# A two-layer trunk: the four shifts of V's first half issued together into two slots, and the first head pair's scores two blocks later

## The chip, the cores and the metric

One core of one Trainium2 chip. The time is that of the device, in microseconds (us), from the first to the last work of one launch; the median of several executions counts. One profiled execution gives the trace from which all durations are read. Engines are named as in the profile: PE multiplies matrices (PEld loads its weights), ACT and DVE work on rows of 128 partitions, POOL fills buffers and issues the shift transfers, SP issues the loads from memory. Each engine takes its instructions strictly in the order in which they stand in its queue.

## The reference

The program is a two-layer trunk over 512 tokens of width 1024. The part that matters here is the token mixer of layer 0, a stick-breaking attention with 16 heads of 64:

```python
def stick_breaking_attention(q, k, v):
    ...
        z = jnp.einsum('bhtd,bhsd->bhts', q[:, :, q0:kend], k[:, :, :kend]) * scale
        before = s_idx < t_idx
        log_beta = jax.nn.log_sigmoid(z)
        log_1m = jnp.where(before, jax.nn.log_sigmoid(-z), 0.0)
        later = lax.cumsum(log_1m, axis=3, reverse=True) - log_1m
        a = jnp.where(before, jnp.exp(log_beta + later), 0.0)
        outs.append(jnp.einsum('bhts,bhsd->bhtd', a, v[:, :, :kend]))

def stick_breaking_mixer(h, w_qkv, w_o):
    qkv = (h @ w_qkv).reshape(B, S, 3, SB_HEADS, SB_HEAD_DIM)
    ...
    return o.transpose(0, 2, 1, 3).reshape(B, S, D) @ w_o
```

Before and after it stand RMS norms with a shift, a scale and a gate computed from a vector `c` (`silu(c) @ w + b`); a SwiGLU, a second mixer and another SwiGLU follow.

## The kernel before

**Numbers.** Every float32 operand of a product is split into a high and a low part (`split`: ACT copies the high part, DVE subtracts it for the low part) and a product is three matmuls (`mm3`: high by high, high by low, low by high). A weight comes from memory as `raw` (512 KB, two buffers), and ACT makes `wh` and DVE `wl` of it (five pairs of buffers). So the next load but one can be issued only when DVE has written `wl` of a weight, and a `wh` can be written only when PE has read the weight five places earlier.

**The stage.** V = h·w_v is made in two halves of 512 columns. Each half has eight steps k (`v_step`: 12 matmuls, four token blocks of three) into four PSUM banks. While the first half is made, so are q and k of the first head pair. After it, `v_evac` copies the four banks to `vf` on ACT. Then comes the second half, again eight steps; then the weights of the further head pairs are used as filler (`fill`: q and k of pair 1, 2, ... in `pqk`, eight steps of three matmuls each), between which the attention of the pairs is spread.

**U.** The sum over values works on differences of neighbouring rows, U[t] = V[t+1] − V[t]. A row lives in a partition, so the shift by a row is a transfer from SBUF to SBUF, issued by POOL: one of 127 rows and, but for the last block, one of the single row from the next block (`shifted`). Then DVE subtracts (`vs<-vs,vf`), ACT writes the high part of U and DVE the low part. Before the change, `u_steps` is a generator with one buffer `vs` for all four blocks, taken in the order 2, 3, 0, 1: a block's shift is issued only when the block before has left the buffer.

**Scores.** `scores` makes z for blocks of keys in three groups (B31: keys 3 and 1, 12 matmuls; B2: six; B0: six) into two banks `zb`. ACT reads them into `ga` (a sigmoid) and DVE runs the scan `left<-ga`. All three groups of pair 0 share the two banks and the one buffer `ga`. The bank `zb[0]` also serves, between B0 and the next pair, the sums of the vectors that scale the norms: `z<-acch`, `z<-accl` (one pair of matmuls for each half of G), after which DVE writes G from the bank. `acch` and `accl` are again a high part by ACT and a low part by DVE, in one buffer each.

**Order.** Python code gives the order in which work is offered; a scheduler then sets each engine's queue. From `pe["chain"]` on, PE keeps the code's order; from `dve.chain` on, so does DVE for all but the weights' `wl`. Before that, a U step is only tied behind the last `wl`. Buffers of 4 KB a partition come from one pool of 28 slots (`slot`), among them U, hT, q, k, `vf`, G and A.

**Names.** A is the next of the scaling vectors: DVE adds `rawada` rows into it, one 512 KB load each, from two buffers; the third and fourth of these loads wait for the first and second sum. In the profile L93 is `mm`, L101 a transpose, L116 and L69 are the two halves of `split` and all other DVE work of the helper, L155/L156 and L160/L161 the `wh`/`wl` of a weight (q and k weights of later pairs, all others), L110 a load by SP, L636/L638 the two shift transfers, L888 the sigmoid.

Of the kernel before, what the change touches and what calls it, by code (L numbers as in the profile page):

```python
# [8 lines left out]
F32 = mybir.dt.float32  # L9
F32R = mybir.dt.float32r  # L10
AF = mybir.ActivationFunctionType
ALU = mybir.AluOpType

P = 128
T = 512
NT = T // P
# [15 lines left out]
def trunk(ctx: ExitStack, tc: tile.TileContext, A: dict, out: bass.AP):  # L32
    nc = tc.nc
# [5 lines left out]
    npool = ctx.enter_context(tc.tile_pool(name="npool", bufs=2))  # L39
# [9 lines left out]
    def nm(s):  # L49
        uid[0] += 1  # L50
        return f"{s}_{uid[0]}"

    def slot(dt, name, a=2, b=512):
        return s4.tile([P, a, b], dt, tag="s4", name=nm(name))

    def bank(name, tag="b"):
        return psum.tile([P, 512], F32, tag=tag, bufs=6 if tag == "b" else 2, name=nm(name))
# [19 lines left out]
    dve = Vector()  # L77
# [7 lines left out]
    def order(b, before):  # L85
        tc.add_manual_dep(
            b.ins, before.ins.name,
            mybir.DependencyInfo(mybir.DependencyClass.NoSync, mybir.DependencyReason.DATA),
            reason="order",
        )  # L90
# [21 lines left out]
    def split(hi, lo, src, hi_dve=False):  # L112
        if hi_dve:
            dve.tensor_copy(hi, src)
        else:
            act.activation(hi, src, AF.Copy)  # L116
        dve.tensor_tensor(lo, src, hi.bitcast(F32), ALU.subtract)
# [6 lines left out]
    last_low = [None]  # L124
# [107 lines left out]
    def wget(src, look=3):  # L232

        n = taken[0]
        taken[0] += 1
        while len(got) < min(n + 1 + look, len(stream)):
            wemit()
        assert stream[n][3] == src, (stream[n][3], src)
        return got[n]
# [336 lines left out]
    def ada_step(n=1):  # L576
        bg.step(bg0.step(n))
# [38 lines left out]
    U = [[slot(F32R, "U", 4, 256) for _ in range(NT)] for _ in range(2)]  # L616

    def v_step(vb, hf, k, w):
        for tt in range(NT):
            a, b = hTk(hT, k, tt * P, P)  # L620
            mm3(vb[tt][:], a, b, w[0][:, k % 2, :], w[1][:, k % 2, :], k == 0, k == KD - 1)

    def v_evac(vb, tile2):
        vf = [tile2() for _ in range(2)]
        vf = [vf[tt // 2][:, tt % 2, :] for tt in range(NT)]
        for tt in range(NT):
            act.activation(vf[tt], vb[tt][:], AF.Copy)
        return vf

    def u_steps(vf, hf, pool):  # L630

        def shifted(tt):
            vs = pool.tile([P, 512], F32, tag="vs", name=nm("vs"))
            if tt == NT - 1:
                nc.gpsimd.memset(vs[96:P, :], 0.0)
            nc.gpsimd.dma_start(out=vs[0 : P - 1, :], in_=vf[tt][1:P, :])  # L636
            if tt < NT - 1:
                nc.gpsimd.dma_start(out=vs[P - 1 : P, :], in_=vf[tt + 1][0:1, :])  # L638
            return vs

        turns = (2, 3, 0, 1)
        vs = shifted(turns[0])
        yield
        for n, tt in enumerate(turns):
            b = dve.tensor_tensor(vs[:], vs[:], vf[tt], ALU.subtract)
            if not dve.chain:
                order(b, last_low[0])
            src = vs[:].rearrange("p (a e c) -> p a e c", a=4, e=2)
            dst = U[hf][tt][:].rearrange("p a (q c) -> p a q c", q=4)
            split(dst[:, :, 0::3, :], dst[:, :, 1:3, :], src)  # L650
            if n + 1 < NT:
                vs = shifted(turns[n + 1])
            yield

    onec = oneb[:, 0:1]

# [72 lines left out]
    vb = [bank("v0") for _ in range(NT)]  # L729
# [37 lines left out]
    st0.__exit__(None, None, None)  # L767
    fwork["raw"] = ctx.enter_context(tc.tile_pool(name="wraw2", bufs=2))
    vf0 = v_evac(vb, lambda: slot(F32, "vf"))
    o8 = []  # L770
    with tc.tile_pool(name="att", bufs=1) as att, tc.tile_pool(name="att2", bufs=2) as att2:

# [49 lines left out]
        def fill(n, at=None):  # L822
            for j in range(n):
                next(fgen, None)
                if at is not None and j in [min(a, n - 1) for a in at]:
                    ada_step()
# [3 lines left out]
        B31, B2, B0 = (3, 1), (2,), (0,)  # L830
        gaps = {}
        for js in (B31, B2, B0):
            at, n = {}, 0
# [118 lines left out]
        evac_k(0, pk0)  # L952
        LATE = ((2, (2,)), (3, (2, 3)))
        EARLY = ((0, (0,)), (1, (0, 1))), ((2, (0, 1)), (3, (0, 1)))
        early_u = u_steps(vf0, 0, att)
        next(early_u)
        vb = [bank("v1") for _ in range(NT)]
        zb = [bank("z") for _ in range(2)]
        bg0.bank = bg.bank = lambda: zb[0]
        cur = attend(0)  # L960
        for k in range(KD):
            if k % 2 == 0:
                wv = wget(("wv", 1, k // 2))
            v_step(vb, 1, k, wv)
            if k in (1, 4):
                cur[0](B31 if k == 1 else B2)
            if k in (1, 2, 6):
                ada_step()
            if k in (3, 5, 7):
                next(early_u)  # L970
        next(early_u)
        late_u = u_steps(
            v_evac(vb, lambda: npool.tile([P, 2, 512], F32, tag="n", name=nm("vf"))), 1, att
        )
        next(late_u)
        dve.chain = True
        tw = [bank("tw") for _ in range(2)]
        av = [bank("av") for _ in range(2)]
# [4 lines left out]
        for i in range(NPAIR):  # L983
            scores, flip, values, gather, part = cur
            more = i + 1 < NPAIR
            F = iter(FILLS if i < 5 else LAST[i - 5])
            flip(LATE, 0)
            flip(LATE, 1)
            if i:
                last_part()  # L990
            fill(next(F))
            if more:
                cur = attend(i + 1)
                cur[0](B31)
            fill(next(F), (1,))
            values(LATE, 0, False)
            values(LATE, 1, False)
            fill(next(F))
            flip(EARLY[0], 0)
            flip(EARLY[0], 1)  # L1000
            if i < 4:
                next(late_u)
            fill(next(F))
            if more:
                cur[0](B2)
            fill(next(F), (1,))
            values(EARLY[0], 0, False)
            values(EARLY[0], 1, False)
            flip(EARLY[1], 0)
            flip(EARLY[1], 1)  # L1010
            fill(next(F))
            if more:
                cur[0](B0)
            fill(next(F), (1,) if i > 3 else ())
            values(EARLY[1], 0, True)
            values(EARLY[1], 1, True)
            gather()
            last_part = part
# [521 lines left out]
```

## Time and profile before

| | us |
|---|---|
| median of 3 runs | 1162.52 |
| lowest, highest | 1162.12, 1162.67 |
| the profiled execution's own time | 1165.49 |
| its span, first to last instruction | 1163.7 |

| engine | busy us | share |
|---|---|---|
| PE | 1126.9 | 97% |
| DVE | 933.8 | 80% |
| ACT | 596.9 | 51% |
| POOL | 30.0 | 3% |

The profiled execution is 3.0 us above the median of the runs; durations come from it. The stage of the change lies between 58 and 131 us of a span of 1163.7 us. A row of the timeline has the start, the duration, engine, line, operation, tiles and, in brackets, how long the engine sat idle before it and what ended that. A matmul's duration is that of its way through the array; the distance of two starts is what it costs in a dense row. The mean granted clock of PE over the span was 0.988.

### The profile page before, as it was taken

To read this page: it belongs to the slowest core of one execution; us is meant where nothing else is said; L and a number is where in the kernel's file an instruction comes from. 1 tells how busy PE (TensorE), PEld (TensorE's weight loads), DVE (VectorE), ACT (ScalarE), POOL (GpSimd) and SP (SyncE) were. 2 spreads that over 40 slices of the span, in tenths; PEclk is the share of its full clock that TensorE was granted. 3 is DMA by queue.
4 is the path that set the end of the run, shared out by engine and by line. 5 is a ranking of instruction groups with operands and counts; after the bars stand their busy time and mean duration, and the time that the engine had idled before them with its cause. 6 is when DMAs were issued, how large, how long until landed. Compare 5 with 4: busy or idle time off the path is not lost.

```text
span 1163.7 us, 18665 instructions
## 1 busy us (share of the span) xinstructions
PE 1126.9 (97%) x7436; PEld 1015.0 (87%) x7436; DVE 933.8 (80%) x1215; ACT 596.9 (51%) x985; POOL 30.0 (3%) x55
## 2 busy tenths in 40 slices
PE   7996899999999999999999999999999999999997
PEld 4774788778999999998878898988999999999996
DVE  4964799975998898879677966668979898789996
ACT  6343456564655555545242643626555555565652
POOL 0101000000000000001000000000000000000000
PEclk9987999999999999999999999999999999999999
DMA  8853624313423444327887465224243433222243
GB/s 327 322 170 121 206 97 138 127 56 127 145 92 128 145 146 145 127 90 258 287 278 244 157 239 170 90 89 156 100 143 130 131 141 128 92 91 91 91 144 111
DMA packets 51644, 176.52 MB, mean 152 GB/s; under 512 B 6106, under 2 KB 9434, under 8 KB 51556
## 3 DMA queue, kind: packets, MB, share of 16 engines
q1 hardware_dynamic: 48996, 166.94, 42.6%
q0 software_dynamic: 2560, 8.39, 1.9%
q8 instruction: 58, 0.95, 0.3%
q14 instruction: 30, 0.25, 0.1%
HBM read 164.82 MB, written 8.39 MB: 149 GB/s over the span
## 4 chain that ended last, share of the span: by engine, by line
PE 80%; DMA 8%; DVE 7%; ACT 3%; issue 2%; SPq 0%; DVEq 0%; POOL 0%; ACTq 0%
PE r L93 32%; PE y L93 8%; PE v L93 8%; PE pqk L93 6%; DMA rawada<-in_ada 5%; PE X L93 4%; PE gu L93 4%; PE Y L93 3%; PE u L93 3%; PE z L93 2%; PE av L93 2%; PE W L93 1%; PE Z L93 1%; PE tw L101 1%; DVE wl L161 1%
## 5 line engine op out<-in xcount | busy, mean ns | idle before, releaser
L93 PE MATMUL r<-Sh,wh 128*128 128x256 f32 x608 | 172.1, 283 | 0.0
L93 PE MATMUL r<-Sl,wh 128*128 128x256 f32 x608 | 172.1, 283 | 0.0
L93 PE MATMUL r<-Sh,wl 128*128 128x256 f32 x608 | 172.1, 283 | 0.0
L93 PE MATMUL y<-wh,as 128*128 128x512 f32 x480 | 150.7, 391 | 0.1
L160 ACT ACTIVATE wh<-raw 128x1024 fp32r<-128x1024 f32 x87 | 91.6, 1058 | 113.3 <-PE y L93 58.3
L161 DVE TENSOR_TENSOR wl<-raw,wh 128x1024 fp32r<-128x1024 f32 x87 | 105.8, 1219 | 43.0 <-ACT wh L160 42.6
L116 ACT ACTIVATE wh<-f 128x1024 fp32r<-128x1024 f32 x87 | 92.2, 1060 | 91.0 <-PE r L93 66.5
L69 DVE TENSOR_TENSOR wl<-f,wh 128x1024 fp32r<-128x1024 f32 x87 | 106.2, 1220 | 40.1 <-ACT wh L116 40.0
L93 PEld LDWEIGHTS r<-Sh,wh 128*128 128x128 f32 x608 | 116.7, 192 | 0.0
L93 PEld LDWEIGHTS r<-Sl,wh 128*128 128x128 f32 x608 | 116.7, 192 | 0.0
L93 PEld LDWEIGHTS r<-Sh,wl 128*128 128x128 f32 x608 | 116.7, 192 | 0.0
L93 PEld LDWEIGHTS y<-wh,as 128*128 128x128 f32 x480 | 90.1, 188 | 18.9 <-DVE G L69 0.5
L93 PE MATMUL y<-wl,as 128*128 128x512 f32 x240 | 93.7, 390 | 0.0
L93 PE MATMUL r<-hTh,wh 128*128 128x256 f32 x304 | 87.8, 292 | 0.0
L93 PE MATMUL r<-hTl,wh 128*128 128x256 f32 x304 | 85.4, 282 | 0.0
L93 PE MATMUL r<-hTh,wl 128*128 128x256 f32 x304 | 81.0, 283 | 0.0
L93 PE MATMUL r<-hTh,b 128*128 128x256 f32 x304 | 61.0, 283 | 0.0
L93 PEld LDWEIGHTS r<-hTh,wh 128*128 128x128 f32 x304 | 58.0, 191 | 2.5 <-DVE gu L69 0.8
L93 PEld LDWEIGHTS r<-hTl,wh 128*128 128x128 f32 x304 | 58.1, 191 | 0.1
L116 ACT ACTIVATE wh<-rawx 128x1024 fp32r<-128x1024 f32 x38 | 40.3, 1060 | 34.7 <-PE r L93 31.8
L93 PEld LDWEIGHTS r<-hTh,wl 128*128 128x128 f32 x304 | 55.9, 191 | 0.0
L93 PE MATMUL v<-wh,hTh 128*128 128x512 f32 x128 | 51.6, 403 | 3.8 <-ACT wh L160 2.0
(268 smaller groups left out, 2986.7 us busy)
## 6 DMA issues: line engine op xcount, KB each, us to landing
rawada<-in_ada SPq DMA_DIRECT2D x80, 512.0 KB, 4.4
rawy<-in_wy SPq DMA_DIRECT2D x38, 512.0 KB, 3.5
rawx<-in_wx SPq DMA_DIRECT2D x38, 512.0 KB, 4.1
raw<-in_wdown SPq DMA_DIRECT2D x22, 512.0 KB, 4.5
raw<-in_wdn SPq DMA_DIRECT2D x22, 512.0 KB, 3.5
raw<-in_wqk SPq DMA_DIRECT2D x16, 512.0 KB, 4.1
ada<-in_ada0p SPq DMA_DIRECT2D x12, 512.0 KB, 8.0
raw<-in_wgu SPq DMA_DIRECT2D x12, 512.0 KB, 3.6
```

Source lines behind the costliest of these rows:

```text
L69: b = getattr(nc.vector, op)(*args, **kw)
L93: b = nc.tensor.matmul(o, l, r, start=start, stop=stop, skip_group_check=True)
L101: last_tp[0] = nc.tensor.transpose(o, i, ident)
L116: act.activation(hi, src, AF.Copy)
L160: act.activation(h[:], raw[:], AF.Copy)
L161: last_low[0] = nc.vector.tensor_tensor(l[:], raw[:], h[:].bitcast(F32), ALU.subtract)
```

## The change

The generator is dissolved into two functions, `shifted` (the transfers of one block) and `u_step` (the subtraction and the split of one block). Three things move:

- For V's first half two more slots of the shared pool hold all four shifted blocks (`vs0`), and all seven transfers are issued in a row right after `v_evac`.
- In V's second half the scores of pair 0 stand after step 3 and step 5 (were 1 and 4), and the four U steps after steps 4, 5, 6 and 7 (were 3, 5, 7 and behind the loop).
- V's second half keeps its one buffer and its order; only the code that says so is another.

```diff
+    TURNS = (2, 3, 0, 1)
+    def shifted(vf, tt, vs):
+        if tt == NT - 1:
+            nc.gpsimd.memset(vs[96:P, :], 0.0)
+        nc.gpsimd.dma_start(out=vs[0 : P - 1, :], in_=vf[tt][1:P, :])
+        if tt < NT - 1:
+            nc.gpsimd.dma_start(out=vs[P - 1 : P, :], in_=vf[tt + 1][0:1, :])
+        return vs
+    def u_step(vf, hf, tt, vs):
+        b = dve.tensor_tensor(vs, vs, vf[tt], ALU.subtract)
...
     vf0 = v_evac(vb, lambda: slot(F32, "vf"))
+    vs0 = [slot(F32, "vs") for _ in range(2)]
+    vs0 = {tt: shifted(vf0, tt, vs0[tt // 2][:, tt % 2, :]) for tt in TURNS}
...
-        early_u = u_steps(vf0, 0, att)
-        next(early_u)
...
-            if k in (1, 4):
-                cur[0](B31 if k == 1 else B2)
+            if k in (3, 5):
+                cur[0](B31 if k == 3 else B2)
             if k in (1, 2, 6):
                 ada_step()
-            if k in (3, 5, 7):
-                next(early_u)
-        next(early_u)
-        late_u = u_steps(
-            v_evac(vb, lambda: npool.tile([P, 2, 512], F32, tag="n", name=nm("vf"))), 1, att
-        )
-        next(late_u)
+            if k > 3:
+                tt = TURNS[k - 4]
+                u_step(vf0, 0, tt, vs0[tt])
+        vf1 = v_evac(vb, lambda: npool.tile([P, 2, 512], F32, tag="n", name=nm("vf")))
+        def shifted1(n):
+            vs = att.tile([P, 512], F32, tag="vs", name=nm("vs"))
+            return shifted(vf1, TURNS[n], vs[:])
+        vs1 = shifted1(0)
...
             if i < 4:
-                next(late_u)
+                u_step(vf1, 1, TURNS[i], vs1)
+                vs1 = shifted1(i + 1) if i < 3 else None
```

ACT's queue at the start of V's second half, from the last `k` of pair 0 on (`acch` is the high part of G's first half, `ga<-z` the sigmoid of the scores B31). Before:

```order
L116 ACTIVATE k_125_623<-pk_75_288 128x512
L116 ACTIVATE acch_170_853<-G_102_455 128x512
L888 ACTIVATE ga_613<-z_131_633 128x128
L888 ACTIVATE ga_613<-z_131_633 128x384
L888 ACTIVATE ga_613<-z_132_634 128x128
L160 ACTIVATE wh_137_643<-raw_136_641 128x1024
L888 ACTIVATE ga_613<-z_132_634 128x384
L160 ACTIVATE wh_140_649<-raw_139_647 128x1024
```

Now:

```order
L116 ACTIVATE k_127_633<-pk_75_288 128x512
L116 ACTIVATE acch_168_851<-G_102_455 128x512
L160 ACTIVATE wh_138_650<-raw_137_648 128x1024
L160 ACTIVATE wh_141_656<-raw_140_654 128x1024
L160 ACTIVATE wh_144_662<-raw_143_660 128x1024
L155 ACTIVATE wh_147_693<-raw_146_691 128x1024
L116 ACTIVATE U_25_139<-vs_118_589 128x4x2x64
L885 ACTIVATE ga_623<-z_132_640 128x128
L885 ACTIVATE ga_623<-z_132_640 128x384
L885 ACTIVATE ga_623<-z_133_641 128x128
L885 ACTIVATE ga_623<-z_133_641 128x384
```

Three of the four sigmoids stood ahead of the weight of steps 2 and 3, and the fourth ahead of that of steps 4 and 5; now the weights of steps 2 to 7, a later one and the first U stand ahead of all four.

DVE's queue up to the scores B0 (`left<-ga` 128x1025) and the writing of G. Before:

```order
L69 TENSOR_TENSOR vs_153_782<-vs_153_782,vf_115_582 128x512
L156 TENSOR_TENSOR wl_180_907<-raw_168_843,wh_179_906 128x1024
L69 TENSOR_TENSOR U_23_137<-vs_153_782,U_23_137 128x4x128
L69 TENSOR_TENSOR vs_157_819<-vs_157_819,vf_115_582 128x512
L69 TENSOR_TENSOR U_24_138<-vs_157_819,U_24_138 128x4x128
L69 TENSOR_TENSOR accl_171_854<-G_102_455,acch_170_853 128x512
L69 SCALAR_TENSOR_TENSOR left_121_616<-ga_613,ones_119_608 128x1025
L69 TENSOR_TENSOR G_102_455<-z_131_633,g_169_851 128x512
```

Now:

```order
L69 TENSOR_TENSOR vs_117_588<-vs_117_588,vf_115_582 128x512
L69 SCALAR_TENSOR_TENSOR left_125_628<-ga_623,ones_120_613 128x513
L69 TENSOR_TENSOR U_24_138<-vs_117_588,U_24_138 128x4x128
L69 TENSOR_TENSOR accl_169_852<-G_102_455,acch_168_851 128x512
L156 TENSOR_TENSOR wl_165_838<-raw_155_790,wh_164_837 128x1024
L156 TENSOR_TENSOR wl_178_905<-raw_166_841,wh_177_904 128x1024
L69 SCALAR_TENSOR_TENSOR left_123_626<-ga_623,ones_121_618 128x1025
L69 TENSOR_TENSOR G_102_455<-z_132_640,g_167_849 128x512
```

The low part `accl` still stands behind the last U, with two weights now between it and the scan of B0.

SP's queue of loads, at G's factor `g` and the start of A. Before:

```order
L110 DMA raw_168_843<-in_wqk 128x1024
L110 DMA raw_181_910<-in_wqk 128x1024
L110 DMA raw_190_956<-in_wqk 128x1024
L110 DMA g_169_851<-in_post_g 128x1024
L110 DMA A_174_888<-in_adab 1x1024
```

Now:

```order
L110 DMA raw_166_841<-in_wqk 128x1024
L110 DMA g_167_849<-in_post_g 128x1024
L110 DMA A_172_886<-in_adab 1x1024
L110 DMA raw_179_908<-in_wqk 128x1024
L110 DMA raw_188_954<-in_wqk 128x1024
```

Two weights (k of pair 3 and q of pair 4) that were loaded ahead of `g` and A now stand behind them; A's load waits for a fill of A that POOL does behind the seven transfers. All else, on every engine from the next head pair on, stands as it stood.

More of the change, by code (lines that the diff above doesn't have):

```diff
@@ L628, in v_evac @@
         return vf
[L630 to L653, printed above, removed]
+    TURNS = (2, 3, 0, 1)
[8 more added lines that the diff above has]
+        b = dve.tensor_tensor(vs, vs, vf[tt], ALU.subtract)
+        if not dve.chain:
+            order(b, last_low[0])
+        src = vs.rearrange("p (a e c) -> p a e c", a=4, e=2)
+        dst = U[hf][tt][:].rearrange("p a (q c) -> p a q c", q=4)
+        split(dst[:, :, 0::3, :], dst[:, :, 1:3, :], src)
     onec = oneb[:, 0:1]
```

## The prediction

> **What bounds the kernel now.** First the page: PE is busy almost throughout, so only time in which PE stands still, or runs at a lower clock, can be won. Then the waits of PE over the whole span, longest first (engine, what it waited for, us in total, times, longest).
>
> ```profile
> span 1163.7 us, 18665 instructions
> PE 1126.9 (97%) x7436; PEld 1015.0 (87%) x7436; DVE 933.8 (80%) x1215; ACT 596.9 (51%) x985; POOL 30.0 (3%) x55
> PE z L93 <- DVE accl L69: 8.6, 1, 8.6
> PE v L93 <- ACT wh L160: 2.0, 1, 2.0
> PE z L93 <- DVE k L69: 1.7, 1, 1.7
> PE z L93 <- ACT ga L888: 1.6, 2, 1.3
> ```
>
> The longest wait of all, for `accl`, lies in the stage that is changed; so do the next two rows and most of the fourth. The timeline of PE tells where, and what it costs.
>
> ```profile
> 67.16 0.39 PE L93 MATMUL v<-wh,hTl 128*128 128x512 f32 x1
> 67.48 1.13 PE L93 MATMUL z<-k,q 64*128 64x128 f32 x12
> 70.60 0.51 PE L93 MATMUL v<-wh,hTh 128*128 128x512 f32 x1 [1.98 <-ACT wh L160]
> 71.86 0.80 PE L93 MATMUL v<-wl,hTh 128*128 128x512 f32 x1 [0.76 <-DVE wl L161]
> 82.58 0.39 PE L93 MATMUL v<-wh,hTl 128*128 128x512 f32 x1
> ...
> 94.77 0.50 PE L93 MATMUL pqk<-hTh,wh 128*128 128x512 f32 x1
> 97.05 0.50 PE L93 MATMUL z<-acch,ones 128*128 128x512 f32 x1 [1.32 <-ACT ga L888]
> 106.12 0.80 PE L93 MATMUL z<-accl,ones 128*128 128x512 f32 x1 [8.57 <-DVE accl L69]
> 108.42 0.63 PE L93 MATMUL pqk<-hTl,wh 128*128 128x512 f32 x1
> 108.85 0.63 PE L93 MATMUL pqk<-hTh,wl 128*128 128x512 f32 x1
> 112.47 0.40 PE L93 MATMUL pqk<-hTh,wh 128*128 128x512 f32 x1
> ```
>
> There are two holes. The first opens after step 1 of V's second half: PE waits 1.98 + 0.76 us for the weight of step 2. The second opens behind the scores B0: 1.32 + 8.57 us. After each, matmuls start 0.43 us apart (108.42 to 108.85) for a while. The chain of waits has the dense distance (24 matmuls in 5.44 us, 0.227 each) and what fed the second hole:
>
> ```profile
> 62.11 5.44 PE v L93 x24
> 67.55 1.10 PE z L93 x12
> 82.97 0.55 PE z L93 x6
> 93.94 0.90 PE z L93 x6
> 95.77 1.22 DVE wl L156
> 97.88 0.53 POOL vs L636
> 98.41 4.86 DMA vs<-vf
> 104.11 0.64 ACT U L116
> 105.39 0.69 DVE accl L69
> 116.58 4.91 DMA rawada<-in_ada
> 122.89 4.96 DMA rawada<-in_ada
> 131.07 1.08 PE av L93 x7
> ```
>
> DVE stands in order: `accl` is behind the fourth U, this behind the fourth shift, and that could be issued (97.88) only when the third U had left the one buffer. The granted clock by stretch (us, busy times of the engines, clock, DMA share, GB/s) shows why the dense rows are slow after a hole:
>
> ```profile
> 61.00:66.00 5.00, 5.00 (x23) 4.14 (x23) 3.68 (x4) 2.22 (x4) 1.17 (x2) 1.00 1.00 373
> 70.00:75.00 5.00, 3.65 (x8) 2.67 (x9) 4.42 (x3) 1.87 (x3) 0.00 (x0) 0.62 0.32 105
> 125.00:130.00 5.00, 4.75 (x20) 3.51 (x20) 2.02 (x2) 2.76 (x6) 0.00 (x0) 0.66 0.50 173
> ```
>
> **What the two holes cost.** First: from 67.39 (67.16 + 0.23) dense work would be 12 scores (about 1.2 us with the change of shape) and three steps at 2.72 (12 x 0.227): end at 76.75. In fact step 4 ended at 82.81 (82.58 + 0.23): **6.06 us**, of which 2.74 are waits and 3.3 slow clock. Second: after 94.77 stand three matmuls (0.81), the pair for G's first half, six, the second pair and six: 16 x 0.227 = 3.63, so 99.21 against 112.47: **13.26 us**, 9.89 of waits and 3.4 of clock. Together 19.3.
>
> The Trainium skill speaks to the clock: "TensorE: Matmul & The Clock Gate", in its table "Why this matters for your kernels", asks for no idle gap over about 3 us and holds that one idle window takes the array to half clock. Here the clock fell to a mean of 0.62 after waits of 1.98 and 0.76 us and to 0.66 after one of 1.7 us, so shorter gaps do it too. By that rule the first hole would have cost its 2.74 us of waits alone and the sum below would be 3.3 us later; I go by the rows.
>
> **The change part by part.** *Removed*: the wait of each shift for the U before it. *Moved*: the scores B31 and B2 (12 and 6 matmuls), the eight U instructions on DVE and the four on ACT, seven POOL transfers, two weight loads on SP. *Added*: nothing but two slots. PE's own work is unchanged. I follow the queues from 64.7 us on, with these rows of ACT and DVE and the landing times of the loads of weights and of the shifts (from issue to landing, lowest/median/highest):
>
> ```profile
> 58.73 0.85 SPq L110 DMA_DIRECT2D raw<-in_wv  x2
> 64.73 0.63 ACT L116 ACTIVATE acch<-G 128x512 fp32r<-128x512 f32 x1 [1.98 <-DVE G L69]
> 69.48 1.07 ACT L160 ACTIVATE wh<-raw 128x1024 fp32r<-128x1024 f32 x1
> 96.42 1.07 ACT L888 ACTIVATE ga<-z 128x512 f32<-128x512 f32 x2
> 105.99 2.29 DVE L69 TENSOR_TENSOR_SCAN left<-ga,ones 128x1025 f32<-128x1025 f32 x1
> 108.19 0.67 DVE L69 TENSOR_TENSOR G<-z,g 128x512 f32<-128x512 f32 x1
> DMA to landing us min/median/max: 3.6/3.8/4.7
> DMA to landing us min/median/max: 2.4/3.2/6.9
> ```
>
> *Steps 2 and 3.* Their weight was loaded with the pair issued at 58.73, so it had landed by 64; only the sigmoids ahead of it on ACT, which waited for the scores, held it to 69.48. Now it follows `acch`, at 65.4 or earlier: `wh` by 66.4, `wl` (1.22) by 67.7. PE wants them at 67.4 and 67.6. The hole closes: steps 2 and 3 end at 72.8, B31 at 74.0, steps 4 and 5 at 79.5, B2 at 80.1, steps 6 and 7 at **85.55**. The next weights, by `wl`, landing (3.8), `wh` (1.07), `wl`: that of steps 6 and 7 by about 73, wanted at 80.1; the first of the filler by 75, wanted at 85.55. Cover enough.
>
> *U and B31, B2.* The seven shifts are issued from 61.0 to about 65 and, at 254 KB each, add 0.76 MB to a DMA that is full there (share 1.00, 373 GB/s in the row above): about 2 us more, all landed by 69 or 70. DVE works off weights, subtractions, Us and the scans of B31 (done near 79) and B2 (near 84); the last U and `accl` end near **85**, 20 us earlier than now (106.08). Nothing of PE waits for a U before 131.07 minus what is won. B31 being two steps later costs nothing: its scan is used only by the first transposes, after the filler.
>
> *Behind V.* ACT copies the four banks by 86.9 and makes one more `wh` by 87.9. PE: three filler steps to 87.6, B0 to 88.6, three matmuls to 89.4. ACT's two sigmoids run from 88.8 to 89.9; PE's `z<-acch` can start after the first, 89.4, and `z<-accl` follows at once, since `accl` is long there. Six matmuls: 91.25. Then **a new wait** takes the place of the old: the second pair needs the bank that DVE empties with `G<-z`, behind the scan of B0. Scan 89.9 to 92.1, G 92.1 to 92.8: PE waits to 92.85, 1.6 us, and 0.4 us more for the second `accl` (92.7 to 93.4). Now the same chain hides behind the slow six matmuls. Six more: the point that is 112.47 now comes at **95.0**. Gain 17.5 us, that is 19.3 minus 2.0, rounded. Bounds for the new waits: nothing (as now) or, should they halve the clock as the 1.7 us wait did, 0.2 x 6 = 1.2 us more in those six matmuls.
>
> *From there to 131.07.* The chain rows show that this stretch is set by DVE and two loads of `rawada` (4.91 and 4.96 us), issued in turn behind DVE's first sums of A, which follow the q that the filler's first eight steps end with. It keeps its 18.6 us; a slow clock in it would be covered by PE's 1.7 us wait for `k`. It could shrink to the loads' 3.6 us: 2.6 us less. Behind it the queues are the same in every row, PE is bound by its own work and the loads follow PE, so the gain stays. The s4 slots: later loads into the two slots (B, x) wait for shifts that landed long before: nothing. V's second half: same instructions, nothing.
>
> **Sum.** 1163.7 − 17.5 = 1146.2 us of span; the profiled execution took 1165.49 around its span, 3.0 above the median of the runs, and the same gain off the median gives 1162.5 − 17.5 = **1145.0 us**.
>
> **The rivals.** (a) *The new wait grows.* The two `wl` now ahead of B0's scan hang on loads that go in a row of three, each issued by the `wl` two before. At the 4.9 us of the `rawada` rows instead of 3.8 the last `wl` ends 3.3 us later, at 92.5 instead of 89.2, the scan starts 2.6 us late and the clock halves (1.2): 1148.8, and 3 us more for each further us of a load. For it: DVE has only 0.7 us in hand there. Against: no other large load runs in that stretch. (b) *The first hole stays*, because the seven shifts crowd the loads: gain 17.5 − 6.1, 1151.1. For it: the DMA's share of 1.00 from 61 to 66, and one shift that took 6.9 us. Against: both weights were issued before the first shift. (c) *Slower*: the shifts are issued in one row, but POOL could hold each until the one before has landed. In the trace a shift of 127 rows and its single row go out 0.5 us apart, never more. At 6.9 us each, seven end at 61 + 48 = 109; the last U on ACT, ahead of the V copies, the next `wh` and B0's sigmoids, would be at 109.7, the sigmoids near 115, the scan 117, G 118, and the 112.47 point near 120: 1170. It decides from 5.6 us each on (last shift at 100.5, as late as the 83 it may come at plus 17.5). The minimum and median of 2.4 and 3.2 speak against it. A's load, behind POOL's fill and now ahead of two weights, would add to it; those weights are wanted from 95 on. (d) *No change*: the scheduler keeps the old order. The printed queues show it does not.
>
> The skill's page "DMA: Bandwidth & Descriptors", section "Queues, rings and completion order", has each DMA engine take turns between the queues it has work for, packet by packet. By that, shifts from POOL's queue would take half the rate from SP's loads, which is (b) again: by this rule, as (b) works out from rows, 1151.1. No run here has had several shifts at once yet.
>
> **How the numbers follow.** The forecast 0.73: 1142.5 (the loads at their fastest) to 1148.5 (clock halved, landings late). (a) 0.13, (b) 0.06, (c) 0.05, (d) 0.03. The range 1142 to 1152 takes in the forecast's own, (a) and (b). What a measurement of this kernel can tell from no change is about 0.2%, 2.3 us: faster 0.73 + 0.13 + 0.06 = 0.92, the same 0.03, slower 0.05.
>
> **What would show it.** Right: no wait of PE for `wh` at step 2 and rows 0.23 us apart through to 85.5; seven shifts issued within 4 us; `accl` done before the scores B0; a wait of PE for G of about 1.6 us; the filler's ninth step near 95; `av` near 113.6. Wrong: a shift issued later than 66, a weight of steps 2 to 7 ending a wait of PE, or an `av` that moved less than the ninth step did.

## The result, and the profile after

The changed kernel took **1150.53 us** (median of 4 runs, 1147.3 to 1151.72) against 1162.6 before (4 runs, 1162.12 to 1166.24): ratio 0.9885, 95% interval 0.9857 to 0.9914, so 12 us won. The forecast was 1145.0 us in a range from 1142 to 1152: the sign and the range held, and the gain came out a third smaller than the 17.5 us it was made of. The time lies above the forecast's own stretch (1142.5 to 1148.5), in the part of the range that was there for the rivals (a) and (b). The profiled execution after took 1150.07 us.

The page of the kernel after, then PE's waits over the whole span, longest first (engine, what it waited for, us in total, times, longest; "..." stands for rows left out):

```profile
span 1148.3 us, 18662 instructions
PE 1121.9 (98%) x7436; PEld 1011.4 (88%) x7436; DVE 933.2 (81%) x1215; ACT 596.6 (52%) x985; POOL 29.9 (3%) x55
```

```profile
PE tp L101 <- DVE x L69: 8.9, 2, 7.3
PE av L93 <- DVE ar L69: 2.4, 1, 2.4
...
PE z L93 <- DVE G L69: 1.5, 1, 1.5
PE z L93 <- ACT ga L885: 1.1, 2, 0.8
...
PE z L93 <- DVE k L69: 0.3, 1, 0.3
```

The wait of 8.6 us for `accl` and the 2.0 for `wh` are gone; a wait for G of 1.5 us is new, as forecast. The longest row, for `x`, lies in the first 11 us of the program. The kernel before has it too, with 8.3 us; the prediction's list passes over it, and over the 1.8 us of `hTh`: not all of the longest waits lie in the stage of the change. PE's timeline after shows where things stand now (first the last product of q in V's first half, which serves below as the mark behind which the change acts):

```profile
61.90 0.39 PE L93 MATMUL pq<-hTh,wh 128*128 128x512 f32 x1
...
86.85 0.39 PE L93 MATMUL v<-wh,hTl 128*128 128x512 f32 x1
...
91.87 0.50 PE L93 MATMUL z<-acch,ones 128*128 128x512 f32 x1 [0.81 <-ACT ga L885]
...
95.52 0.47 PE L93 MATMUL z<-acch,ones 128*128 128x512 f32 x1 [1.51 <-DVE G L69]
...
97.70 0.63 PE L93 MATMUL pqk<-hTh,wl 128*128 128x512 f32 x1
98.13 0.63 PE L93 MATMUL pqk<-hTh,wh 128*128 128x512 f32 x1
...
116.01 1.08 PE L93 MATMUL av<-ar,U 128*128 128x128 f32 x7 [2.36 <-DVE ar L69]
116.93 0.40 PE L93 MATMUL pqk<-hTh,wh 128*128 128x512 f32 x1
```

V's second half runs without a gap and ends at 87.08 (86.85 + 0.23). Then come a wait of 0.81 us for the sigmoids of B0, which the forecast had at nothing, and the wait for G; from 97.30 on, 1.8 us after the end of that wait, rows stand 0.43 us apart (97.70 to 98.13): half clock. The shifts on POOL, and DVE around B0, in their timelines:

```profile
62.33 0.67 POOL L636 DMA_DIRECT2D vs<-vf  x1 [3.10 <-ACT vf L627]
...
65.59 0.50 POOL L638 DMA_DIRECT2D vs<-vf  x1
```

```profile
88.27 0.69 DVE L69 TENSOR_TENSOR accl<-G,acch 128x512 fp32r<-128x512 f32 x1
...
92.51 2.29 DVE L69 TENSOR_TENSOR_SCAN left<-ga,ones 128x1025 f32<-128x1025 f32 x1
94.71 0.67 DVE L69 TENSOR_TENSOR G<-z,g 128x512 f32<-128x512 f32 x1
```

Seven transfers leave in 3.8 us (62.33 to 66.09), and `accl` is done at 88.96, ahead of the scores B0 (89.21). The chain of waits of the kernel after names what is late instead:

```profile
67.87 6.61 DMA raw<-in_wv
...
76.85 3.46 DMA raw<-in_wqk
...
83.72 3.65 DMA raw<-in_wqk
...
90.27 1.08 ACT wh L155
...
92.51 2.29 DVE left L69
...
108.36 4.42 DMA rawada<-in_ada
```

The weight of V's steps 6 and 7 (the load at 67.87) took 6.61 us to land where 3.8 was reckoned. PE did not wait for it, but the later weights follow it through their buffers, and one `wh` (90.27) stands ahead of the sigmoids of B0.

**Where the time went.** One profile of each kernel is not enough for this. The mark (61.90 after, 60.59 before) moves from one execution to the next, and so does what lies behind it. Here are four profiles of the kernel before and three of the one after, each worked out from the starts of the same matmuls in the trace, in us behind the mark: the filler's ninth step (the point 112.47 of the prediction), the first `av` group that waits (131.07 there), and the end of the span.

| execution | mark | ninth step | `av` | end |
|---|---|---|---|---|
| before, as in the prediction | 60.59 | 51.88 | 70.48 | 1103.1 |
| before, second to fourth | 61.67, 61.58, 61.29 | 49.90, 50.13, 49.20 | 68.01, 67.76, 66.97 | 1102.0, 1100.4, 1098.1 |
| after | 61.90 | 36.23 | 54.11 | 1086.4 |
| after, second and third | 64.41, 59.58 | 36.59, 37.05 | 53.96, 54.99 | 1087.8, 1091.9 |
| mean before | 61.28 | 50.28 | 68.31 | 1100.9 |
| mean after | 61.96 | 36.62 | 54.35 | 1088.7 |
| won | | **13.7** | **14.0** | **12.2** |

The means give 12.2 us at the end, as the medians do. The single pair of profiles would have given 15.4 (1163.7 to 1148.3).

### The profile page after: what moved, and what is told of

The parts are those of the page before. It is cut to its first block, busy times and chain, and to the rows that moved or that the text cites. A ratio compares the mean times of both kernels' runs of the same rounds, so it can differ in the third digit from the quotient of the medians.

```text
span 1148.3 us, 18662 instructions
## 1 busy us (share of the span) xinstructions
PE 1121.9 (98%) x7436; PEld 1011.4 (88%) x7436; DVE 933.2 (81%) x1215; ACT 596.6 (52%) x985; POOL 29.9 (3%) x55
## 4 chain that ended last, share of the span: by engine, by line
PE 76%; DMA 11%; DVE 8%; ACT 3%; issue 2%; SPq 0%; DVEq 0%; ACTq 0%
PE r L93 32%; PE y L93 10%; PE pqk L93 6%; DMA rawada<-in_ada 6%; PE gu L93 5%; PE X L93 4%; PE Y L93 3%; PE v L93 2%; PE u L93 2%; PE av L93 2%; PE z L93 2%; PE W L93 1%; PE Z L93 1%; PE tw L101 1%; DMA raw<-in_wv 1%
## 5 line engine op out<-in xcount | busy, mean ns | idle before, releaser
L69 DVE TENSOR_TENSOR wl<-rawx,wh 128x1024 fp32r<-128x1024 f32 x38 | 46.5, 1223 | 10.2 <-ACT wh L116 10.2
```

Source lines behind the costliest of these rows:

```text
L69: b = getattr(nc.vector, op)(*args, **kw)
```

## The experiments

**The two kernels again.** No edit. The kernel of the change, in another series of runs:

> The changed kernel once more, unaltered, for its own spread. If the spread of its first runs (1147.3 to 1151.7) comes from where the half-clock stretches of PE fall behind short waits, the spans of the single runs again differ by several us and go with the mean granted clock (0.001 of clock is about 1.1 us); if it was that one chip, they agree within 0.5 us. Median 1149 to 1151.

Measured 1152.08 us (5 runs, 1151.1 to 1153.94) against 1164.16 before: ratio 0.9894 [0.9875, 0.9913], 12 us again, though above the 1149 to 1151 expected. The single runs do not go with their clock: the fastest and the slowest, 2.8 us apart, both have 0.995. The kernel before, and then both once more, each with a single run and its profile:

> The kernel before, unaltered, profiled once more. The question is how much of the 15.4 us between the two profiled spans (1163.7 and 1148.3) belongs to the change. Up to the last product of q and k in V's first half (60.59 us before, 61.90 after; four later profiles of after and its variants: 64.41, 60.68, 61.37, 64.72) both kernels run the same instructions, so that point should scatter from one execution to the next. Theory one (the start is scatter, the change acts behind that point): here it stands anywhere from 60 to 65, and the rest of the span, 1103.1 us in the profile before, comes out between 1101 and 1105. Theory two (the change itself makes the start later): it stands at 60.6 again, within 0.3, in this and every profile of before. Theory three (the first profile of before was a slow one behind that point too): the rest is 1100 or less.

> The kernel before once more. Both profiles of it so far took 1165.4 us, above the median of its other runs (1162.5 and 1163.8), with the last product of q and k in V's first half at 60.59 and 61.67. If the start is scatter of the execution (60.3 to 64.7 over ten profiles), it stands in that range here, and what lies behind it comes to 1102 to 1103 us again. If the part behind it scatters too, by the length of slow clock after the two holes, it lies between 1097 and 1103.

> As the third profile of the kernel before: with both, the mean of what lies behind the start is known to about 1 us. With 1087 us for the kernel of the change a mean of 1102.5 makes the gain 15.5 us; a mean of 1099 makes it 12, as the medians have it.

> The kernel of the change once more: the start anywhere from 60.3 to 64.7, what lies behind it 1086 to 1088 us as in the two profiles so far (1086.4 and 1087.8). The waits as there: about 0.7 us for the sigmoids of B0, 1.5 for G, 2.4 for ar before the first av, and rows 0.43 us apart behind the wait for G and behind that for ar.

The rows are in the table above. The second profile of before, with 1102.0 us behind the mark, fits the first of its theories; the third and fourth, with 1100.4 and 1098.1, show that the part behind the mark scatters too. The mark lay between 59.58 and 64.72 over all fourteen profiles taken, without order by kernel: that the change makes the start later is not borne out. What lies behind the mark scatters by 5 us in either kernel; the third profile of after, at 1091.9, lies outside what was expected. Part of this scatter is in the length of half clock behind a wait, as PE's timeline of that third execution shows at `av`:

```profile
114.57 1.86 PE L93 MATMUL av<-ar,U 128*128 128x128 f32 x7 [2.66 <-DVE ar L69]
...
116.65 0.63 PE L93 MATMUL pqk<-hTl,wh 128*128 128x512 f32 x1
117.08 0.63 PE L93 MATMUL pqk<-hTh,wl 128*128 128x512 f32 x1
```

Rows are 0.43 us apart behind a wait of 2.66 us here, for six microseconds in all, and 0.23 behind the 2.36 us in the profile shown first (116.93, next 117.16). In the second profile five rows are 0.43 us apart behind a wait of 2.33 us.

**The scores alone.** The kernel before with one edit:

```diff
-            if k in (1, 4):
-                cur[0](B31 if k == 1 else B2)
+            if k in (3, 5):
+                cur[0](B31 if k == 3 else B2)
```

> The kernel before with only the scores of the first pair moved to steps 3 and 5 of V's second half; the shifts still go one after another through one buffer. If the two holes are independent, the first closes (no wait of PE for wh at step 2, rows 0.23 us apart there) and the second keeps its 13.3 us: 6 us faster than before. The rival: the chain of shift, subtraction, U and next shift then runs on its own clock, four shifts of 3 to 5 us with about 3 us of DVE, ACT and POOL between them, and PE comes to it 6 us earlier: the wait for accl grows by what the first hole gave, and the kernel gains 0 to 2 us. The weight of steps 6 and 7, with two shifts and the loads of A beside it in place of seven, should land in 3.6 to 5 us; at 6.6 the shifts are not what made it slow.

1156.36 us (6 runs) against 1163.83: ratio 0.9929 [0.9904, 0.9953], 8 us won; behind the mark the profiled execution has the ninth step at 41.44 and ends at 1091.9, 9 us before the mean of before. That is more than either expectation. PE's waits behind B0 in its timeline, and POOL's shifts:

```profile
95.46 0.49 PE L93 MATMUL z<-acch,ones 128*128 128x512 f32 x1 [1.97 <-ACT ga L888]
...
99.37 0.80 PE L93 MATMUL z<-accl,ones 128*128 128x512 f32 x1 [3.42 <-DVE accl L69]
```

```profile
80.81 0.56 POOL L636 DMA_DIRECT2D vs<-vf  x1 [0.30 <-POOL vs L635]
87.06 0.54 POOL L636 DMA_DIRECT2D vs<-vf  x1 [5.69 <-DVE U L69]
...
93.54 0.54 POOL L636 DMA_DIRECT2D vs<-vf  x1 [5.45 <-DVE U L69]
```

The first hole is closed, and the second shrinks from 8.57 to 3.42 us of wait although the shifts still go one by one. They leave 16.7, 22.9 and 29.4 us behind the mark (64.14); before it was 21.8, 28.7 and 37.3 (82.38, 89.28 and 97.88 less 60.59). With the steps of V on time the Us come on time, and the shifts with them: the load of the last weight of V, which the Us follow, is issued 7.0 us behind the mark (71.14) where it was 11.2 (71.83 less 60.59). The second hole was in part the first one's echo.

**The early shifts alone.** The changed kernel with `(3, 5)` back at `(1, 4)`, the edit above turned round.

> The kernel of the change with the scores of the first pair back at steps 1 and 4: only the early shifts and the two slots are left of it. If the holes are independent, the first is there again (a wait of PE of 2 to 3 us for wh and wl at step 2 and half clock behind it, 6 us) and the second is closed: 6 us slower than the kernel of the change, some 7 to 10 us faster than before. The rival, that seven shifts at once make the loads late however the scores stand: the weights of V's steps wait longer than before, and less than 4 us of gain over before is left. accl is done before the scores B0 in either case.

1155.72 us (6 runs): ratio 0.9926 [0.9904, 0.9947], 8 us won, within the 7 to 10 expected; it is some 4 us slower than the kernel of the change, where 6 were expected. Behind the mark (60.32) its profile, that of the fastest of the six runs, has the ninth step at 39.27 and the end at 1090.7. PE's timeline:

```profile
70.33 0.49 PE L93 MATMUL v<-wh,hTh 128*128 128x512 f32 x1 [1.98 <-ACT wh L160]
...
71.59 0.79 PE L93 MATMUL v<-wl,hTh 128*128 128x512 f32 x1 [0.77 <-DVE wl L161]
...
97.34 0.47 PE L93 MATMUL z<-acch,ones 128*128 128x512 f32 x1 [1.44 <-DVE G L69]
...
98.19 0.40 PE L93 MATMUL pqk<-hTh,wh 128*128 128x512 f32 x1
98.43 0.40 PE L93 MATMUL pqk<-hTl,wh 128*128 128x512 f32 x1
```

The waits of the first hole are back, to within 0.01 us, and the wait for `accl` is gone. At the ninth step 11.0 us are won (50.28 less 39.27); the prediction's terms give 17.5 − 6.06 = 11.4 for this half of the change. That only 8 are left in the median of the runs is not explained. Alone the edits win 8 us each, together 12.

**A's first loads behind the weights.** What delays the weight of steps 6 and 7? The changed kernel with A's first two `rawada` loads, which were issued just ahead of the shifts, ordered behind the weight that follows the delayed one, the filler's first:

```diff
-                        load(raw, A["ada"][s, part, k])
+                        ld = load(raw, A["ada"][s, part, k])
+                        if (name, at, k) in (("A", 0, 0), ("A", 0, 1)):
+                            order(ld, behind[10])
```

(`behind` lists the loads of weights in their order.)

> The changed kernel with the first two loads of A (512 KB each, wanted only at 100 us) issued behind the load of the first filler weight instead of just before the seven shifts. My theory: the load of the weight of steps 6 and 7 took 6.6 us because A's loads and the shifts share the DMA with it; without A's loads it lands within 5 us, the scan of B0 starts 1 us or more earlier, the 0.8 us wait of the first acch matmul goes, and the time is 1 to 2 us less than that of the changed kernel. Rival: the shifts alone fill the DMA, the load still takes over 6 us and the time is the same within 0.5 us.

1150.09 us (5 runs, 1146.07 to 1151.01) against 1152.08 for the unaltered kernel of the change on that chip: ratio to before 0.9864 [0.984, 0.9887]. All five runs lie below all five of that kernel, though by 0.1 us at the nearest, and the two intervals overlap. SP's timeline, ACT's, and PE's say what moved:

```profile
66.60 0.33 SPq L110 DMA_DIRECT2D raw<-in_wv  x1
```

```profile
70.19 1.06 ACT L161 ACTIVATE wh<-raw 128x1024 fp32r<-128x1024 f32 x1 [3.93 <-DMA raw<-in_wv]
```

```profile
93.14 0.47 PE L93 MATMUL z<-acch,ones 128*128 128x512 f32 x1 [1.38 <-DVE G L69]
93.64 0.50 PE L93 MATMUL z<-accl,ones 128*128 128x512 f32 x1
93.97 0.39 PE L93 MATMUL pqk<-hTh,wh 128*128 128x512 f32 x1
94.20 0.39 PE L93 MATMUL pqk<-hTl,wh 128*128 128x512 f32 x1
```

The weight lands in under 3.6 us (66.60 to 70.19) instead of 6.61. The seven shifts, issued in the same way, land 3.1 to 3.9 us after issue, where in the kernel of the change they took 7.8 to 8.4 (the transfers' landing times in the two traces: 62.33 to 70.20 for the first there, 61.12 to 64.76 here). Over 64 to 72 us the DMA's share is 0.98 and 1.05 there (four microseconds each), 0.69 and 0.77 here. So it is the shifts together with A's two loads of 512 KB that fill the DMA. With the scores alone moved, so with two shifts and A's loads, the same weight was issued at 71.14 and its `wh` began at 74.65; but the two shifts landed by 71.86, so that load had hardly anything beside it. The wait for the sigmoids of B0 is gone (the 0.3 us of that name that this kernel has left are elsewhere), the scan of B0 begins 29.4 us behind the mark (90.11 less 60.68) instead of 30.6, the wait for G stays at 1.38, and no slow rows follow: the ninth step comes 34.65 us behind the mark instead of 36.6.

**The second pair of G's sums two filler steps later.** If the wait for G is what halves the clock, PE should do filler in it (the next step of the same work, which stood behind filler step 4, moves to 5):

```diff
-            fill(n, (0, 2, 4, 6))
+            fill(n, (0, 4, 5, 6) if n == 8 else (0, 2, 4, 6))
```

> The changed kernel with the second pair of matmuls of G's sums two filler steps later (12 filler matmuls between the pairs instead of 6). My theory: the wait of PE for G (1.5 us) was the last wait before the filler's ninth step; it goes, and with it the half clock behind it: ninth step 2 to 2.5 us earlier against the end of V, and because q and with it A's two loads follow that step, av comes as much earlier and the time is 1.5 to 2.5 us less. Rival: the time from the ninth step to av is not tied to that step but to A's loads by themselves, so PE only waits longer for av: same within 0.5 us.

1147.99 us (4 runs, 1147.32 to 1149.39): ratio 0.9858 [0.9837, 0.9879], 4.1 us below the kernel of the change on the same chip, and no overlap of the two ranges. That is more than the 1.5 to 2.5 expected: at the ninth step the profile is 2.2 us ahead of the mean of after, as expected, at the end (1084.4) 4.3, and where the rest comes from is not shown. PE's timeline:

```profile
91.28 0.50 PE L93 MATMUL z<-acch,ones 128*128 128x512 f32 x1 [0.74 <-ACT ga L885]
...
94.93 0.47 PE L93 MATMUL z<-acch,ones 128*128 128x512 f32 x1 [0.16 <-DVE G L69]
```

The wait for G is 0.16 us and the slow rows behind it are gone: the ninth step stands at 34.41 behind the mark, by chance just where the forecast had it (95.0 − 60.59). The 0.74 us for the sigmoids alone slowed nothing.

**Both edits.**

> Both edits: A's loads later and the second pair two steps later. If the two are separate costs, 2.5 to 4.5 us less than the changed kernel (near 1147). If both feed the same wait (the chain from the weights' loads through DVE to G), no more than the better of the two alone.

1149.61 us (5 runs, 1146.38 to 1150.18): ratio 0.9863 [0.984, 0.9887]. By the trace it is the better of the three at the ninth step (33.29 behind the mark) and at the end (1083.1, against 1084.1 and 1084.4), by the runs it is not told apart from them, so they do not show whether the two savings add. The mark of the profiled run was at 64.72, the latest of all.

**Two sums of A fewer before the first `av`.** The prediction held that the stretch from the ninth step to `av` is set by A's loads and sums. In the kernel with both edits, two sums go from the last nine filler steps into the first two head pairs:

```diff
-            fill(n, (0, 4, 5, 6) if n == 8 else (0, 2, 4, 6))
+            fill(n, (0, 4, 5, 6) if n == 8 else (0, 4))
...
-            fill(next(F))
+            fill(next(F), (1,) if i < 2 else None)
```

> The changed kernel with A's loads behind the weights, the second pair of G's sums two filler steps later, and two of the four sums of A in the last nine filler steps before the first av put off into the first two head pairs. If the stretch to av is set by A's loads and sums on DVE, PE's wait for ar (1.8 us in the version without the last edit) and the slow clock behind it go, the wait for k (0.9) too: 2 to 4 us faster than that version (1149.6), about 1146. If another chain is right behind it (the transposes and scans of the first pair), the wait stays within 0.5 us of 1.8 and the time is the same. If the sums put off come to stand before something that PE waits for, later waits appear in the first two pairs and the gain is given back.

> The kernel of the change with the second pair of G's sums two filler steps later and two of the four sums of A before the first av put off; A's loads stand where the change has them. If A's loads ahead of the weights cost only the 0.8 us wait for the sigmoids of B0 once the pair is later, this is within 1 us of the version with all three edits (1142.6): 1143 to 1144. If they still make a wait that halves the clock, it is 2 to 4 us slower than that: 1145 to 1147.

The first took 1142.61 us, with both earlier edits (4 runs, 1141.08 to 1145.58; ratio 0.9821 [0.9794, 0.9848]), where 1146 was expected; the second 1143.77, with the later pair of G alone (5 runs, 1141.88 to 1145.64; ratio 0.9823 [0.9795, 0.9851]), as expected. These are the two fastest versions, and where A's loads stand makes no difference that these runs tell. PE's timeline of the second of them:

```profile
96.03 0.47 PE L93 MATMUL z<-acch,ones 128*128 128x512 f32 x1 [0.18 <-DVE G L69]
...
107.19 1.13 PE L93 MATMUL z<-k,q 64*128 64x128 f32 x12
...
110.42 1.08 PE L93 MATMUL av<-ar,U 128*128 128x128 f32 x8
```

The waits for `k` and `ar` are gone, `av` comes 48.3 us behind the mark (54.35 after the change, 51.36 with the later pair of G alone), and the clock is 1.00 throughout:

```profile
94.00:106.00 12.00, 11.78 (x55) 9.27 (x54) 9.97 (x11) 3.49 (x5) 0.00 (x0) 1.00 0.63 195
106.00:118.00 12.00, 12.00 (x75) 9.64 (x74) 10.57 (x12) 5.38 (x13) 0.00 (x0) 1.00 0.60 208
```

(The row's columns are as in the prediction's stretches: busy us of PE, PEld, DVE, ACT and POOL, clock, DMA share, GB/s.)

## Why the prediction was right, and where its size was off

**The mechanism held, step by step.** The first hole closed: no wait of PE for a weight from step 2 on, V's second half over 25.18 us behind the mark (87.08 − 61.90) where 24.96 was forecast (85.55 − 60.59). The second closed: seven shifts in 3.8 us, `accl` ahead of B0, if 2.7 us later than forecast (27.1 us behind the mark for 24.4). The new wait for G came in the place named and of the size named (1.51, 1.55 and 1.55 us in three profiles; 1.6 forecast). The stretch from the ninth step to `av` kept its length: 18.0 us mean before (68.31 − 50.28), 17.7 after (54.35 − 36.62), and A set it, as two sums fewer showed. None of the signs named as "wrong" appeared; of those named as "right", the ninth step and `av` came late (96.8 and 114.7 on the prediction's clock, 36.23 and 54.11 + 60.59, for 95 and 113.6).

**Three terms of the sum were mis-sized**, and with the stretch they make up 5.2 of the 5.5 us between 1145.0 and 1150.5:

- *What the two holes cost, 1.6 too many* (51.88 us to the ninth step in the one execution they were read from, 50.28 in the mean of four). Worked out as the prediction does, the first hole cost 6.06, 4.68, 6.09 and 4.51 us in the four executions, the second 13.26, 12.66, 11.48 and 12.12: 0.7 of the 1.6 is in the first term, 0.9 in the second. The waits hardly differ (2.74 or 2.75 us in the first hole, 9.3 to 10.2 in the second); most of it is the slow clock behind them, which lasted 14 rows after each hole in the execution of the prediction and 6 to 14 in the others. The execution was known to be 3 us above the median; the forecast took the gain from it all the same and set it off against the median.
- *The ninth step at 95.0, 2.2 too early* (34.41 behind the mark; 36.62 measured). The forecast had the seven shifts landed by 69 or 70, 9.4 us behind the mark at most, and the loads behind them at 3.8 us; the last shift landed at 73.70, 11.8 behind it. The weight that landed in 6.61 us passed its delay on, so the sigmoids of B0 came late (0.81, 0.63 and 0.67 us of PE's time) and the scan with them; with A's loads out of the way both came as forecast (no wait, the scan at 29.4). The wait for G ended 1.3 us later than forecast in the mean of the three; the clock that halved behind it makes up the other 0.9. The forecast had given this 1.2 us as a bound only.
- *"The gain stays" behind `av`, 1.7 too many* (14.0 won at `av`, 12.2 at the end). It rests on the third profile of after, which took 1036.9 us from `av` to the end; the other two took 1032.3 and 1033.8, the four of before 1031.1 to 1034.0. Half clock behind the wait for `ar` is part of it: none in the first profile of after, two microseconds in the second, six in the third. How much of the 1.7 is this and how much the scatter of later stages, seven profiles do not settle.
- The stretch from the ninth step to `av`, 0.3 us shorter than before in the means, goes the other way.

**The rivals.** (a) The new wait grows through the chain of weights: in part. The scan of B0 began 30.6 us behind the mark (92.51 − 61.90); the forecast had 29.3 (89.9 − 60.59) and (a) 31.9 (92.5 − 60.59). But PE came late as well, held by the same chain at the sigmoids, so the wait for G itself did not grow; the clock did halve, as (a) had it. (b) The first hole stays because the shifts crowd the loads: its 1151.1 is nearest to the time, but not for its reason. The crowding was there, 6.61 us for a load beside the shifts and A's two loads against 3.6 without the two, but it fell on a weight that PE wanted only at 81.6 (87.08 less two steps), since those of steps 2 to 5 had been issued ahead of the shifts. This is also what became of the rule of the Trainium skill's page "DMA: Bandwidth & Descriptors" (section "Queues, rings and completion order"), by which queues take turns on each DMA engine: a load beside the shifts and A's loads was slowed, which agrees with it, but no run here shows the turns themselves. (c) POOL holding each shift until the last has landed: refuted, seven leave 0.5 to 0.7 us apart (in the trace before, too, the first two are 0.66 us apart, not 0.5). (d) No change: refuted.

**The two holes were not independent.** The sum treated 6.06 and 13.26 us as two losses that add up. Worked out in the same way, moving the scores alone took away the first hole (5.3 us in the mean of before, 0.3 left) and also 3.8 us of the second (12.4 in the mean, 8.6 left). At the ninth step the two edits alone won 8.8 (50.28 less 41.44) and 11.0 us, both together 13.7: some 6 us of it can be had only once. In the medians the overlap is smaller, 8 and 8 against 12, and within their intervals. For the forecast, which was of both edits, this does no harm.

## What to carry to other kernels

Before a gain is summed up from a profile, look how far the same point of the program stands from the start in several executions: here the two holes together were 2.7 us longer in one than in another (51.88 to 49.20), beside a forecast gain of 17.5. A wait that is a few microseconds long costs what it lasts and, now and then, as much again in slow clock behind it; moving independent work into it (the pair of G's sums two steps later) won more than the wait itself here. And look at what large loads are in flight when several transfers are issued at once: here the seven were harmless by themselves, and beside two loads of 512 KB they delayed a third, which cost PE nothing at that weight and something later, through the buffers that the next loads share with it.

## What the runs showed of the hardware that was not expected

The clock does not follow the length of the last wait alone. In PE's timelines of two executions of the kernel before, the wait for `k` ahead of the second `z<-k,q` is 1.47 us in the fourth and 1.52 us in the second:

```profile
122.58 1.25 PE L93 MATMUL z<-k,q 64*128 64x128 f32 x10 [1.47 <-DVE k L69]
...
124.36 0.63 PE L93 MATMUL pqk<-hTl,wh 128*128 128x512 f32 x1
124.78 0.63 PE L93 MATMUL pqk<-hTh,wl 128*128 128x512 f32 x1
```

```profile
123.70 1.02 PE L93 MATMUL z<-k,q 64*128 64x128 f32 x10 [1.52 <-DVE k L69]
...
124.98 0.39 PE L93 MATMUL pqk<-hTl,wh 128*128 128x512 f32 x1
125.22 0.39 PE L93 MATMUL pqk<-hTh,wl 128*128 128x512 f32 x1
```

The shorter one halved the clock (0.42 us from row to row), the longer did not (0.24). Likewise 2.36 us at `av` left the clock alone in the first profile of after, 2.33 in the second halved it for five rows and 2.66 in the third for six microseconds; a wait for G of 1.38 or 1.44 us by itself did nothing, while 1.51 to 1.55 us some 3 us behind one of 0.6 to 0.8 halved it in all three profiles of after. What decides between them stays open. The Trainium skill's "TensorE: Matmul & The Clock Gate" asks, in its table "Why this matters for your kernels", for no gap over about 3 us; by these rows gaps of half that length are already a risk, if not a certainty.

The start of the program scatters by 5 us: the mark lay between 59.58 and 64.72 us in fourteen executions with the same instructions ahead of it. Most of that is there early: PE's 31st matmul starts between 14.71 and 18.19 us, in nearly the same order of executions, and in the four with the latest mark the mean clock from 30 to 40 us is 0.83 to 0.89, against 1.00 in the other ten. So times of this kernel that are less than some 4 us apart need several runs each, and differences in a trace are better taken from a mark than from zero.
